# Retention's last transposes eight filler steps later, and a PSUM bank for the value products in layer 1's last stage

## The chip, the cores and the metric

The kernel runs on one core of a Trainium2 chip. The metric is the device time of one execution in microseconds; the time before is the median of three runs, 1503.15 us (1498.87 to 1505.15).

The core has five engines, each with an instruction stream of its own: TensorE (PE in the profile; its weight loads are PEld), VectorE (DVE), ScalarE (ACT), GpSimd (POOL), and SyncE (SP), which here issues nearly all DMA transfers. An engine that comes to an instruction whose inputs or whose buffer is not ready waits, and what stands behind it on that engine waits too. TensorE writes its results to PSUM, eight banks here of 128 x 512 floats; VectorE or ScalarE must take a result out ("evacuate" it) before the bank can serve again.

## What is computed

A two-layer encoder trunk over 1,024 prompt tokens and 512 sample tokens, width 1,024, in float32. Layer 0 has two mixers side by side: dense attention (8 heads, 2 key/value heads, with rotary positions) and retention (4 heads, forward and backward scan over 128-token chunks). Layer 1 is windowed attention (16 heads, tokens within 128 of each other, a relative-position bias and a sink logit). Each branch is multiplied by a SiLU gate and goes through one output projection to the residual.

```python
def attn_retention_layer(x, g, w_in, qk_gain, ret_decay, w_out):
    z = rmsnorm(x, g) @ w_in
    qa, ka, va, ga, qb, kb, vb, gb = jnp.split(z, cuts, axis=-1)
    ...
    oa = dense_gqa(qa, ka, va)
    fwd = retention(qb, kb, vb, log_gamma[0], True)
    bwd = jnp.flip(retention(jnp.flip(qb, 1), jnp.flip(kb, 1), jnp.flip(vb, 1), log_gamma[1], False), 1)
    ob = rmsnorm(fwd + bwd, None)
    mixed = jnp.concatenate([jax.nn.silu(ga) * oa, jax.nn.silu(gb) * ob], axis=-1)
    return x + mixed @ w_out

def windowed_layer(x, g, w_in, sink, rel_bias, w_out):
    z = rmsnorm(x, g) @ w_in
    q, k, v, gate = jnp.split(z, [...], axis=-1)
    o = banded_sink_gqa(q, k, v, sink, rel_bias)
    return x + (jax.nn.silu(gate) * o) @ w_out
```

## The kernel before

**Tiling.** The 1,536 tokens are 12 blocks of 128 (`NB`): blocks 0 to 7 are the prompt, 8 to 11 the sample. Four blocks are a group `t` (`GB` = 4, `NG` = 3), worked on in the order 2, 0, 1 (`ORDER`). Activations stand transposed in SBUF as `X["h", k, t]` and `X["l", k, t]`, a rounded high part and the remainder, for each of 8 slices `k` of the model width; a float32 product is made of three products of such parts. Every matmul is issued by the helper `mm` at line 89, every transpose by line 173, so the profile tells them apart by tiles, not by lines.

**Stages.** Key and value projections; retention, head by head; layer 0's attention; layer 0's output projection, begun inside the attention's last units; layer 1's key/value projection; layer 1's attention; layer 1's output projection, begun in the same way. The last two are what "layer 1's last stage" means below: it lies from about 1299 us on.

**Retention.** `retention(h, w, b0, b1)` projects and rotates a head's queries, keys and values and returns `retain`, which is called one step later as `last()`: it runs the scan over the chunk states (`stt`), and for each group of four blocks makes the products `po` (line 644 on), ScalarE squares them (`sq`), VectorE sums the squares (`ssa`, line 650), GpSimd raises to the power -1/2 (`rstd`, line 103), VectorE scales (`on`, line 653), TensorE transposes (`pto`), ScalarE copies (`oT`, line 658) and SP stores it in HBM. The last `retain`, of head 3 on the sample, is `tail`, and is called inside the attention, by `begin`.

**Fillers.** Both attentions run in `pipeline`: for each unit (a block of queries for four heads) `front` makes scores (`s` in layer 0, `sc` in layer 1) and softmax weights; `Back.T` transposes the weights (`pte`) and splits them (`eh`, `el`); `Back.PV` makes the value products (`po`). Between them `Fill.step` puts in fillers, pieces of projections that are independent of the attention. In layer 0 they are first the query projections of heads 4 to 7 (`q_pieces_a`): eight pieces fill one PSUM tile `psq` for a pair of blocks, and with the eighth the pair's rope step is written: copies on ScalarE (line 479), a sum of squares and three wide passes on VectorE (lines 425, 427, 433, 434), a power and two products on GpSimd (lines 103, 430), and stores. Then come the gates (`psg`), and in each layer's last stage the output projection (`pso`, in `out_proj_fm`): 24 matmuls into one PSUM tile, then `y`, VectorE's addition of the residual (line 283), which evacuates it.

`begin` is called by `pipeline` when the first unit's scores are written: it writes `PRE_A` = 23 fillers, then `tail()`, then `POST_A` = 2.

**PSUM banks.** Five of the eight banks are one ring with the tag `s` (scores, transposes, retention's `po` and `pto`); the other three have the tags `pj0` to `pj2` and are given out by `ps_p` in turn, to fillers (`use="fill"`) and to the value products (`use="out"`):

```python
    ring = dict(all=[0, 1, 2], fill=[0, 1, 2], out=[0, 1, 2], i=0)

    def ps_p(name, use="fill"):
        free = ring[use]
        ring["i"] = next(i % 3 for i in range(ring["i"] + 1, ring["i"] + 4) if i % 3 in free)
        return pp.tile([P, 512], F32, tag=f"pj{ring['i']}", name=name, bufs=1)
```

In layer 0's attention `fill` is `[0, 1]` and `out` is `[2]`; in layer 1 all three serve both.

**What sets the order.** The program is written once, in the order of the code, and a scheduler (the tile framework's, with a model of times) then puts each engine's instructions into the order in which they run: of those that it holds to be ready, the one written first, and `tc.high_priority()` lifts a few. A tile that draws on a ring of buffers must wait for the earlier user of its buffer. A filler that `paced` writes also keeps behind an earlier `pte`.

Of the kernel before, what the change touches and what calls it, by code (L numbers as in the profile page):

```python
# [10 lines left out]
AF = mybir.ActivationFunctionType  # L11
# [11 lines left out]
GB = 4  # L23
# [5 lines left out]
PRE_A = 23  # L29
# [7 lines left out]
def trunk_kernel(ctx, tc, x, xT, wab, woab, wc, woc, gT, qkg, ret, sink, relb, fng,  # L37
                 ropeA, ropeB, dist, kdist, qdist, onehot, wmask, out_p0, out_p1, out_s):
    nc = tc.nc
    dma = nc.sync.dma_start  # L40
# [12 lines left out]
    def buf(tag, name, n=None, dt=F32):  # L53
        t = wk.tile([P, SIZE[tag]], dt, tag=tag, name=name, bufs=BUFS[tag])
        return t if n is None else t[:, :n]
# [4 lines left out]
    def ps_t(name):  # L60
        return pp.tile([P, 512], F32, tag="s", name=name, bufs=5)

    ring = dict(all=[0, 1, 2], fill=[0, 1, 2], out=[0, 1, 2], i=0)
# [9 lines left out]
    def small(name, n, bufs=2):  # L73
        return st.tile([P, n], F32, tag=name, name=name, bufs=bufs)
# [13 lines left out]
    def mm(ps, lhsT, rhs, start, stop):  # L88
        i = nc.tensor.matmul(ps, lhsT=lhsT, rhs=rhs, start=start, stop=stop)  # L89
        if pace["after"] is not None:  # L90
            tc.add_manual_dep(i.ins, pace["after"], order, reason="a filler keeps to its place in the pipeline")
            pace["after"] = None
        return i
# [78 lines left out]
    def transpose(o, i):  # L172
        return nc.tensor.transpose(o, i, ident)  # L173
# [145 lines left out]
    def drain(gens):  # L319
        while gens:  # L320
            for _ in gens.pop():
                pass
# [30 lines left out]
    def scratch(name):  # L353
        return [[dr.tile([P, 512], F32, name=f"{name}{k}{t}")[:] for t in range(NG)] for k in range(KT)]

    o_ab, g_ab, o_c, g_c = scratch("oab"), scratch("gab"), scratch("oc"), scratch("gc")
# [210 lines left out]
    def v4(t):  # L567
        return t.rearrange("p (b i) -> p b i", b=GB)
# [65 lines left out]
    def retain(h, b0, n, parts, tiles, stt, kvs):  # L634
        for i in range(n - 1):
            nc.vector.scalar_tensor_tensor(stt[0:64, i + 1, :], stt[0:64, i, :], cdec[0:64, h:h + 1],
                                           kvs[i // GB][0:64, i % GB, :], ALU.mult, ALU.add)
            j = n - 1 - i
            nc.vector.scalar_tensor_tensor(stt[64:128, j - 1, :], stt[64:128, j, :], cdec[64:128, 4 + h:5 + h],
                                           kvs[j // GB][64:128, j % GB, :], ALU.mult, ALU.add)  # L640
        for i0, (vs, qfb, sT) in zip(parts, tiles):
            po = ps_t("po")
            pov = v4(po)
            for j in range(GB):
                mm(pov[:, j, :], sT[:, j, :], vs[j], True, False)
                mm(pov[:, j, :], qfb[:, j, :], stt[:, i0 + j, :], False, True)
            sq = buf("O", "sq")
            nc.scalar.activation(sq, po, AF.Square)
            ss = small("ssa", 8)[:, :GB]
            nc.vector.tensor_reduce(ss, v4(sq), AX.X, ALU.add)  # L650
            r = rstd_of(ss, P, GB)
            on = v4(buf("O", "on"))
            nc.vector.tensor_tensor(on, pov, r.unsqueeze(2).to_broadcast([P, GB, P]), ALU.mult)
            pt = ps_t("pto")
            for j in range(GB):
                transpose(v4(pt)[:, j, :], on[:, j, :])
            oT = buf("H", "oT")
            nc.scalar.activation(oT, pt, AF.Copy)
            dma(out=o_ab[4 + h][(b0 + i0) // GB], in_=oT)

    def bias_table():
        oh = buf("H", "oh")
# [8 lines left out]
        dma(out=brow_d, in_=wm[:16])  # L671
        dma(out=btab_d, in_=bass.AP(brow_d.tensor, brow_d.offset, [[512, 16], [0, P], [1, 512]]))

    tail = lambda: None
    for h in range(4):
        w = ws[h]
        if h < 3:
            ws.append(load_w(wab, h + 1, "w" if h % 2 else "wg"))
        for (b0, b1) in SEQS:
            tail, last = retention(h, w, b0, b1), tail  # L680
            last()
            if 1 <= 2 * h + (b0 > 0) <= NB // 2:
                q_late(PAIRS[2 * h + (b0 > 0) - 1])

# [210 lines left out]
    fill = Fill(fill_a(), 240 / 110.0)  # L895

    def begin():
        for _ in range(PRE_A):
            fill.one()
        tail()  # L900
        for _ in range(POST_A):
            fill.one()

# [32 lines left out]
    for i in (1, 0):  # L936
        KH, KL, V = seq_tiles(F32R, "KH", "KL", "V")
        for t in ORDER:
            pt = ps_t("ptk")
# [143 lines left out]
    def hook_c(u):  # L1083
        c, b = u
        if c == 3 and b in (BLOCKS[GB], BLOCKS[2 * GB]):
            t = 2 if b == BLOCKS[GB] else 0
            for _ in fillc.gates:
                pass
            if t == 2:
                late.clear()  # L1090
            drain(ahead)
            drain([mix_fm(t, KS_C if t else KS_C[6:], o_c, g_c)])
            ahead.append(mix_fm(0 if t else 1, KS_C[:6], o_c, g_c))
            fillc.more.append(out_proj_fm(t, woc, KS_C, lambda k: x1T_d[k][t], x2T_d, fin_out, None if t else late, nc.vector, t == 0))
# [2 lines left out]
             lambda kb, n: 4 if kb == n - 1 else 0, lambda n: 3.5, fillc, hook_c)  # L1097
    drain(ahead)
    fillc.rest()

    fn = buf("S4", "fn")
    dma(out=fn, in_=bcast(fng, D))
# [103 lines left out]
```

## Time and profile before

| | |
|---|---|
| median of three runs | 1503.15 us |
| lowest, highest | 1498.87, 1505.15 us |
| profiled execution, its own time | 1498.49 us |
| profiled execution, span | 1496.4 us |
| TensorE, share of the span busy | 96% |
| VectorE | 70% |
| GpSimd | 54% |
| ScalarE | 48% |

The profiled execution is a single one, shorter than the median of the runs by 4.7 us; the durations of the rows below are of it alone. A row of the timeline merges neighbouring instructions of one kind (x4); its duration runs from the first's start to the last's end, and since matmuls overlap in the pipeline, the start of the next row, and not the end of this one, tells how long TensorE was taken up. In brackets stands the idle time of the engine ahead of the row and what ended it. A wait in the view of waits is such idle time, summed for one pair of a waiting tile and its releaser.

### The profile page before, as it was taken

The numbers are of one execution on the slowest core, as the hardware profiler recorded it, in microseconds if no ns is written. First come the engines' busy times: TensorE is split into PE (matmuls) and PEld (weight loads), VectorE is DVE, ScalarE is ACT, GpSimd is POOL, SyncE is SP. The second block draws the span as 40 slices with busy tenths as digits, with TensorE's granted clock in tenths as the row PEclk, the third lists the DMA queues.
The fourth block names the chain that finished last, engine by engine and source line by source line (L and its number), as shares of the span: only waits on it lengthen the run. The fifth ranks groups of instructions, "written<-read, shape, count | busy, mean of one in ns | idle before, by whom it ended". The sixth has DMA issues, their size and how long they took to land.

```text
span 1496.4 us, 25439 instructions
## 1 busy us (share of the span) xinstructions
PE 1444.0 (96%) x8446; PEld 1250.3 (84%) x8446; DVE 1050.6 (70%) x2431; ACT 722.8 (48%) x1782; POOL 813.0 (54%) x1044
## 2 busy tenths in 40 slices
PE   8999999999999999989998999999999999999997
PEld 6899999977888887878777998888888888776787
DVE  6466776686666667877978137687777767888774
ACT  5542232364555555555652245565555556645202
POOL 7654664474646575886986433442622532566552
PEclk9999999999999999999999999999999999999999
DMA  9541221326212243543664231221212211567752
GB/s 327 186 147 53 79 57 61 100 74 198 75 50 63 62 119 125 199 142 106 201 207 142 71 119 37 61 78 47 78 40 92 67 51 54 171 209 261 247 166 98
DMA packets 138355, 176.55 MB, mean 118 GB/s; under 512 B 38064, under 2 KB 68784, under 8 KB 138224
## 3 DMA queue, kind: packets, MB, share of 16 engines
q1 hardware_dynamic: 136064, 169.41, 35.9%
q0 software_dynamic: 2016, 5.51, 1.2%
q8 instruction: 67, 1.10, 0.3%
q14 instruction: 64, 0.52, 0.1%
q10 hardware_dynamic: 144, 0.01, 0.0%
HBM read 125.83 MB, written 53.25 MB: 120 GB/s over the span
## 4 chain that ended last, share of the span: by engine, by line
PE 75%; DVE 9%; DMA 6%; POOL 4%; issue 3%; ACT 2%; SPq 0%; POOLq 0%; DVEq 0%; ACTq 0%
PE psg L89 17%; PE psq L89 11%; PE pso L89 9%; PE po L89 9%; PE psb L89 8%; PE pte L173 7%; PE s L89 4%; PE sc L89 4%; PE pskv L89 2%; DVE xl L118 2%; PE pskq L89 2%; DVE w L140 1%; DMA mo<-gab 1%; DMA wraw<-in_woc 1%; PE ptq L173 1%
## 5 line engine op out<-in xcount | busy, mean ns | idle before, releaser
L89 PE MATMUL psg<-xh,wg 128*128 128x512 f32 x768 | 263.4, 400 | 0.4 <-POOL wg L139 0.4
L107 POOL TENSOR_SCALAR ec<-ec,rl 128x384 f32<-128x384 f32 (+1 forms) x192 | 107.9, 576 | 242.3 <-DVE rl L1068 86.3
L112 DVE TENSOR_TENSOR el<-pte,eh 128x512 fp32r<-128x512 f32 x288 | 196.5, 685 | 56.0 <-ACT eh L111 32.4
L111 ACT ACTIVATE eh<-pte 128x512 fp32r<-128x512 f32 x288 | 169.7, 596 | 116.2 <-PE po L89 64.5
L89 PE MATMUL pso<-xh,w 128*128 128x512 f32 x512 | 179.3, 409 | 8.4 <-DVE w L140 3.2
L89 PEld LDWEIGHTS psg<-xh,wg 128*128 128x128 f32 x768 | 143.6, 188 | 28.5 <-POOL wg L139 0.8
L107 POOL TENSOR_SCALAR e<-e,rl 128x512 f32<-128x512 f32 x160 | 117.1, 744 | 87.2 <-DVE rl L860 28.4
L89 PE MATMUL psg<-xl,wg 128*128 128x512 f32 x384 | 150.8, 393 | 0.0
L1063 ACT ACTIVATE ec<-ec,nm 128x384 f32<-128x384 f32 (+1 forms) x192 | 109.6, 572 | 82.3 <-DVE nm L1061 77.4
L857 ACT ACTIVATE e<-s,nm 128x512 f32<-128x512 f32 x160 | 108.8, 686 | 70.8 <-DVE nm L854 51.2
L849 DVE TENSOR_REDUCE nm<-s 128x1 f32<-128x512 f32 x160 | 107.6, 682 | 36.6 <-PE s L89 36.2
L89 PE MATMUL psq<-xh,w 128*128 128x512 f32 x384 | 129.9, 397 | 0.6 <-DVE oT L719 0.6
L139 POOL TENSOR_SCALAR w<-wraw 128x512 fp32r<-128x512 f32 x112 | 75.9, 679 | 90.3 <-PE pskv L89 32.0
L89 PEld LDWEIGHTS pso<-xh,w 128*128 128x128 f32 x512 | 96.7, 192 | 32.9 <-DVE w L140 5.7
L1057 DVE CUSTOM_DVE_ANT_0 ec<-sc,bias,sink_s 128x384 f32<-128x384 f32 (+1 forms) x192 | 105.2, 569 | 22.1 <-PE sc L89 18.2
L89 PE MATMUL pso<-xl,w 128*128 128x512 f32 x256 | 102.5, 402 | 1.6 <-DVE xl L118 1.6
L173 PE MATMUL pte<-ident,e 128*128 128x128 f32 x640 | 95.2, 274 | 1.5 <-ACT e L857 1.3
L173 PEld LDWEIGHTS pte<-ident,e 128*128 128x128 f32 x640 | 78.6, 141 | 19.8 <-ACT e L857 2.9
L140 POOL TENSOR_TENSOR w<-wraw,w 128x512 fp32r<-128x512 f32 x64 | 84.6, 1325 | 1.7
L89 PEld LDWEIGHTS psq<-xh,w 128*128 128x128 f32 x384 | 71.9, 188 | 14.3 <-PE po L89 0.8
L89 PEld LDWEIGHTS psg<-xl,wg 128*128 128x128 f32 x384 | 72.3, 188 | 13.1
L173 PE MATMUL pte<-ident,ec 128*128 128x128 f32 x512 | 78.9, 272 | 0.1
(234 smaller groups left out, 3891.7 us busy)
## 6 DMA issues: line engine op xcount, KB each, us to landing
wraw<-in_woab SPq DMA_DIRECT2D x48, 256.0 KB, 3.3
wraw<-in_woc SPq DMA_DIRECT2D x48, 256.0 KB, 3.9
wraw<-in_wab SPq DMA_DIRECT2D x44, 256.0 KB, 3.4
wraw<-in_wc SPq DMA_DIRECT2D x36, 256.0 KB, 3.1
xt<-in_xT SPq DMA_DIRECT2D x24, 256.0 KB, 5.7
xb<-in_x SPq DMA_DIRECT2D x24, 256.0 KB, 4.0
qd<-qd SPq DMA_DIRECT2D x48, 128.0 KB, 3.0
gab<-gz SPq DMA_DIRECT2D x24, 256.0 KB, 2.0
```

The costliest lines, as they stand in the source:

```text
L89: i = nc.tensor.matmul(ps, lhsT=lhsT, rhs=rhs, start=start, stop=stop)
L107: nc.gpsimd.tensor_scalar(o, i, s, 1.0, ALU.mult, ALU.mult)
L111: nc.scalar.activation(hi, src, AF.Copy)
L112: nc.vector.tensor_tensor(lo, src, hi.bitcast(F32), ALU.subtract)
L118: nc.vector.scalar_tensor_tensor(lo, src, scale, hi.bitcast(F32), ALU.mult, ALU.subtract)
L139: nc.gpsimd.tensor_scalar(w[:, 0, :], raw, 1.0, 1.0, ALU.mult, ALU.mult)
L140: (lo or nc.gpsimd).tensor_tensor(w[:, 1, :], raw, w[:, 0, :].bitcast(F32), ALU.subtract)
L173: return nc.tensor.transpose(o, i, ident)
L849: nc.vector.tensor_reduce(nm2[:, c:c + 1] if nh == 2 else nm[:, h:h + 1], s, AX.X, ALU.max, negate=True)
L857: nc.scalar.activation(eh[c], ss[c], AF.Exp, bias=nm[:, h:h + 1], accum_out=l[:, h, c:c + 1])
L1057: nc.vector.tensor_tensor_reduce(es[h][:, :nk], s, bias[h][:, bo:bo + nk], 1.0, sink_s[:, 4 * c + h:4 * c + h + 1], ALU.add, ALU.max, mx[: ...
L1063: nc.scalar.activation(es[a][:, :nk], es[a][:, :nk], AF.Exp, bias=nm[:, a:a + 1], accum_out=l[:, a:a + 1])
```

## The change

It has two edits. The first: where `retain` works on one group of four blocks (the sample), it no longer writes the transposes, the copy and the store, but returns a function that does (`flip`); with two groups (the prompt) all is written as before. `begin` writes 15 fillers, `tail()`, eight fillers, the postponed transposes, and the two fillers as before. For the other heads' samples the returned function is called at once.

The second: in `hook_c`, which runs in the first unit of each token group, for head group 3 and the token group behind the sample, the ring is set to `fill=[0, 1]`, `out=[2]`, and back to three for both when the attention and its fillers are done.

```diff
--- before.py
+++ after.py
@@ -638,6 +638,7 @@
             j = n - 1 - i
             nc.vector.scalar_tensor_tensor(stt[64:128, j - 1, :], stt[64:128, j, :], cdec[64:128, 4 + h:5 + h],
                                            kvs[j // GB][64:128, j % GB, :], ALU.mult, ALU.add)
+        done = []
         for i0, (vs, qfb, sT) in zip(parts, tiles):
             po = ps_t("po")
             pov = v4(po)
@@ -651,12 +652,18 @@
             r = rstd_of(ss, P, GB)
             on = v4(buf("O", "on"))
             nc.vector.tensor_tensor(on, pov, r.unsqueeze(2).to_broadcast([P, GB, P]), ALU.mult)
-            pt = ps_t("pto")
-            for j in range(GB):
-                transpose(v4(pt)[:, j, :], on[:, j, :])
-            oT = buf("H", "oT")
-            nc.scalar.activation(oT, pt, AF.Copy)
-            dma(out=o_ab[4 + h][(b0 + i0) // GB], in_=oT)
+            done.append((i0, on))
+            if len(parts) > 1:
+                flip(h, b0, *done.pop())
+        return lambda: [flip(h, b0, *d) for d in done]
+
+    def flip(h, b0, i0, on):
+        pt = ps_t("pto")
+        for j in range(GB):
+            transpose(v4(pt)[:, j, :], on[:, j, :])
+        oT = buf("H", "oT")
+        nc.scalar.activation(oT, pt, AF.Copy)
+        dma(out=o_ab[4 + h][(b0 + i0) // GB], in_=oT)
 
     def bias_table():
         oh = buf("H", "oh")
@@ -671,14 +678,14 @@
         dma(out=brow_d, in_=wm[:16])
         dma(out=btab_d, in_=bass.AP(brow_d.tensor, brow_d.offset, [[512, 16], [0, P], [1, 512]]))
 
-    tail = lambda: None
+    tail = lambda: lambda: None
     for h in range(4):
         w = ws[h]
         if h < 3:
             ws.append(load_w(wab, h + 1, "w" if h % 2 else "wg"))
         for (b0, b1) in SEQS:
             tail, last = retention(h, w, b0, b1), tail
-            last()
+            last()()
             if 1 <= 2 * h + (b0 > 0) <= NB // 2:
                 q_late(PAIRS[2 * h + (b0 > 0) - 1])
 
@@ -895,9 +902,12 @@
     fill = Fill(fill_a(), 240 / 110.0)
 
     def begin():
-        for _ in range(PRE_A):
+        for _ in range(PRE_A - 8):
             fill.one()
-        tail()
+        flips = tail()
+        for _ in range(8):
+            fill.one()
+        flips()
         for _ in range(POST_A):
             fill.one()
 
@@ -1088,6 +1098,7 @@
                 pass
             if t == 2:
                 late.clear()
+                ring.update(fill=[0, 1], out=[2])
             drain(ahead)
             drain([mix_fm(t, KS_C if t else KS_C[6:], o_c, g_c)])
             ahead.append(mix_fm(0 if t else 1, KS_C[:6], o_c, g_c))
@@ -1097,6 +1108,7 @@
              lambda kb, n: 4 if kb == n - 1 else 0, lambda n: 3.5, fillc, hook_c)
     drain(ahead)
     fillc.rest()
+    ring.update(fill=[0, 1, 2], out=[0, 1, 2])
 
     fn = buf("S4", "fn")
     dma(out=fn, in_=bcast(fng, D))
```

Where the two edits move instructions, in the order built from the code:

TensorE, where retention's last products meet their transposes (`po` products, `pto` their transposes, `pte` and `ptq` those of attention weights and queries, `s` scores), before:

```order
L89 MATMUL po<-z,sT 128x128
L89 MATMUL po<-stt,qfb 128x128
L173 MATMUL pto<-ident,on 128x128 x4
L173 MATMUL pte<-ident,e 128x128 x4
L173 MATMUL ptq<-ident,qd 128x128 x4
L89 MATMUL s<-ak,qh 128x512
L89 MATMUL s<-ak,ql 128x512
```

and after:

```order
L89 MATMUL po<-z,sT 128x128
L89 MATMUL po<-stt,qfb 128x128
L173 MATMUL pto<-ident,on 128x128 x4
L173 MATMUL pte<-ident,e 128x128 x4
L173 MATMUL ptq<-ident,qd 128x128 x4
L89 MATMUL s<-ak,qh 128x512
L89 MATMUL s<-ak,ql 128x512
```

Nothing moved here: the transposes follow the products at once in both, and the rows ahead, fillers, are the same too.

VectorE at that place (`ssa` sums of squares, of retention's `sq` and of the fillers' `zq`; `ms` the mean; `on` the scaled product that `pto` transposes), before:

```order
L650 TENSOR_REDUCE ssa<-sq 128x4
L425 TENSOR_REDUCE ssa<-zq 128x8
L100 TENSOR_SCALAR ms<-ssa 128x4
L100 TENSOR_SCALAR ms<-ssa 128x8
L425 TENSOR_REDUCE ssa<-zq 128x8
L100 TENSOR_SCALAR ms<-ssa 128x8
L653 TENSOR_TENSOR on<-po,rstd 128x512
L427 TENSOR_TENSOR zq<-zq,rstd 128x512 x2
L112 TENSOR_TENSOR el<-pte,eh 128x512
```

and after:

```order
L651 TENSOR_REDUCE ssa<-sq 128x4
L425 TENSOR_REDUCE ssa<-zq 128x8
L100 TENSOR_SCALAR ms<-ssa 128x4
L100 TENSOR_SCALAR ms<-ssa 128x8
L425 TENSOR_REDUCE ssa<-zq 128x8 x2
L100 TENSOR_SCALAR ms<-ssa 128x8
L654 TENSOR_TENSOR on<-po,rstd 128x512
L100 TENSOR_SCALAR ms<-ssa 128x8
L427 TENSOR_TENSOR zq<-zq,rstd 128x512 x2
L112 TENSOR_TENSOR el<-pte,eh 128x512
L856 TENSOR_REDUCE nm<-s 128x1
```

One reduction for a filler group (line 425), which stood further up, now stands ahead of `on`, and the group's other passes (lines 427, 433, 434) behind it.

TensorE in layer 1's last stage, at the first two projections of the output (`pso_15933` and `pso_16039`; `po_15967` value products, `sc` scores), before:

```order
L89 MATMUL pso_16039<-xl42_15800,w_15923 128x512
L89 MATMUL pso_15933<-xh42_15799,w_15923 128x512
L89 MATMUL pso_15933<-xh52_15807,w_15923 128x512
L89 MATMUL pso_16039<-xh42_15799,w_15923 128x512
L89 MATMUL sc_16004<-ch0_13657,qs3_15072 128x384
L89 MATMUL po_15967<-eh_15894,cv0_13971 128x512
L89 MATMUL sc_16004<-cl0_13659,qs3_15072 128x384
L89 MATMUL pso_15933<-xl52_15808,w_15923 128x512
L89 MATMUL pso_15933<-xh52_15807,w_15923 128x512
L89 MATMUL pso_16039<-xh52_15807,w_15923 128x512
```

and after:

```order
L89 MATMUL pso_15933<-xl72_15824,w_15928 128x512
L89 MATMUL pso_15933<-xh72_15823,w_15928 128x512
L89 MATMUL po_15967<-eh_15975,cv0_13971 128x512
L89 MATMUL sc_16130<-ch0_13657,qs1_15510 128x384
L89 MATMUL sc_16130<-cl0_13659,qs1_15510 128x384
L89 MATMUL po_15967<-el_15976,cv0_13971 128x512
L89 MATMUL sc_16143<-ch0_13657,qs2_15511 128x384
L89 MATMUL sc_16143<-cl0_13659,qs2_15511 128x384
L89 MATMUL pso_16039<-xh02_15767,w_15913 128x512
L89 MATMUL pso_16039<-xl02_15768,w_15913 128x512
```

Before, the matmuls of the two projections are woven into each other; after, the second begins when the first has ended, two value products and four scores later. From TensorE's instructions near 345 us to those near 1298 us the two orders are the same.

## Rows read from the trace of the kernel before

**Rows 1.** The page's first lines: the span, and each engine's busy time.

```profile
span 1496.4 us, 25439 instructions
...
PE 1444.0 (96%) x8446; PEld 1250.3 (84%) x8446; DVE 1050.6 (70%) x2431; ACT 722.8 (48%) x1782; POOL 813.0 (54%) x1044
```

**Rows 2.** TensorE's waits, whole span: in total, times, longest, all in us.

```profile
PE pto L173 <- DVE on L653: 4.0, 1, 4.0
...
PE po L89 <- DVE y L283: 1.9, 1, 1.9
...
PE pso L89 <- DVE oT L719: 0.9, 1, 0.9
...
PE pso L89 <- DVE y L283: 0.6, 2, 0.3
```

**Rows 3.** Busy time by stretch: length, then PE, PEld, DVE, ACT, POOL; clock; DMA.

```profile
305.00:345.00 40.00, 38.53 (x236) 32.54 (x235) 37.79 (x83) 26.41 (x64) 30.03 (x36) 1.00 0.32 87
1290.00:1330.00 40.00, 34.83 (x155) 27.31 (x154) 39.08 (x87) 22.49 (x56) 28.25 (x30) 0.91 0.73 238
1320.00:1330.00 10.00, 7.82 (x23) 5.62 (x24) 9.66 (x20) 4.02 (x7) 5.38 (x7) 0.66 0.68 213
```

**Rows 4.** Timeline of TensorE: start, us, instruction, [idle before it <- releaser].

```profile
286.20 0.60 PE L173 MATMUL pto<-ident,on 128*128 128x128 f32 x4
...
301.97 1.12 PE L173 MATMUL pto<-ident,on 128*128 128x128 f32 x4 [3.98 <-DVE on L653]
```

**Rows 5.** Timeline of VectorE, the retention's end and behind it.

```profile
283.85 0.69 DVE L425 TENSOR_REDUCE ssa<-zq 128x8 f32<-128x512 f32 x1 [0.37 <-ACT zq L423]
...
301.22 0.69 DVE L653 TENSOR_TENSOR on<-po,rstd 128x512 f32<-128x512 f32 x1 [0.28 <-POOL rstd L103]
...
319.69 0.69 DVE L112 TENSOR_TENSOR el<-pte,eh 128x512 fp32r<-128x512 f32 x1 [1.24 <-ACT eh L111]
```

**Rows 6.** Timeline of GpSimd, beside it.

```profile
300.16 4.24 POOL L103 TENSOR_TENSOR rstd<-ms,nhalf 128x4 f32<-128x4 f32 x3 [1.48 <-DVE ms L100]
```

**Rows 7.** Timeline of TensorE, layer 1's last stage, first part.

```profile
1316.30 0.39 PE L89 MATMUL pso<-xh,w 128*128 128x512 f32 x1
...
1318.12 0.39 PE L89 MATMUL pso<-xh,w 128*128 128x512 f32 x1
...
1323.01 0.76 PE L89 MATMUL po<-eh,cv 128*128 128x512 f32 x1 [1.85 <-DVE y L283]
...
1327.97 1.05 PE L89 MATMUL pso<-xh,w 128*128 128x512 f32 x2
...
1330.66 0.62 PE L89 MATMUL pso<-xh,w 128*128 128x512 f32 x2
1331.11 0.39 PE L89 MATMUL pso<-xl,w 128*128 128x512 f32 x1
```

**Rows 8.** Timeline of VectorE there: the evacuations `y` of five projections.

```profile
1322.17 0.69 DVE L283 TENSOR_TENSOR y<-pso,y 128x512 f32<-128x512 f32 x1
...
1324.88 0.68 DVE L283 TENSOR_TENSOR y<-pso,y 128x512 f32<-128x512 f32 x1
...
1355.66 0.68 DVE L283 TENSOR_TENSOR y<-pso,y 128x512 f32<-128x512 f32 x1
...
1369.01 0.68 DVE L283 TENSOR_TENSOR y<-pso,y 128x512 f32<-128x512 f32 x1
...
1378.19 0.68 DVE L283 TENSOR_TENSOR y<-pso,y 128x512 f32<-128x512 f32 x1
```

**Rows 9.** Timeline of TensorE, second part of that stage.

```profile
1351.00 0.39 PE L89 MATMUL pso<-xh,w 128*128 128x512 f32 x1
...
1362.62 0.39 PE L89 MATMUL pso<-xh,w 128*128 128x512 f32 x1
...
1368.46 1.04 PE L173 MATMUL pte<-ident,ec 128*128 128x128 f32 x8
...
1374.15 0.40 PE L89 MATMUL pso<-xh,w 128*128 128x512 f32 x1
```

## The prediction

> **What bounds the kernel now.** I read the page first: TensorE is busy 1444.0 of 1496.4 us [rows 1], so a gain can only come from its idle time and from stretches where it runs at the lower clock. The view of TensorE's waits comes next; the reader is to look for the waits that the two edits name. The longest single one of a transpose is retention's `pto`, 4.0 us behind VectorE's `on`; then come `po` behind `y` with 1.9, `pso` behind `oT` with 0.9 and `pso` behind `y` with 0.6 in two waits [rows 2]. The first belongs to edit 1; 1.9, 0.9 and one 0.3 of the 0.6 belong to the last stage of layer 1, edit 2. Last, the busy times by stretch. From 305 to 345 us VectorE works 37.79 of 40 us, and from 1290 to 1330 39.08 of 40 [rows 3]: behind both places VectorE is nearly as full as TensorE, so what is taken from a TensorE wait there may be met again as a wait for VectorE.
>
> **Edit 1: the transposes eight fillers later.** The code asks for 15 fillers, products, 8 fillers, transposes. The built order does not give that: on TensorE `po` and `pto` still stand next to each other, and what stands ahead of them is the same. The scheduler places what is ready, and the fillers are ready before the products. So the 3.98 us of idle ahead of `pto` stay, and so does the lower clock behind it: four transposes take 1.12 us there against 0.60 at 286.20 [rows 4]. Nothing is removed.
>
> What does move is the vector work of one filler group (the rope step of the second pair of query blocks). It stood on VectorE from 283.85 on, in a stretch with room; now it stands behind retention's sum of squares, since the group's last filler is written after the products, and both draw `ssa` tiles from one ring of two, which I take to be the reason. It is four wide instructions of about 0.69 us (the first at 283.85) and one tiny one: 4 x 0.69 = 2.8 us, on VectorE; on GpSimd a power `rstd` of 4.24 / 3 = 1.4 us [rows 5, 6] and two products. Its two stores to HBM leave SP's queue earlier in order and enter it later; the loads `qd` behind them come sooner, and none of the transposes that wait for `qd` near there is late by more than 0.3 us.
> - Ahead of `on` stands one more reduction of 0.69 us; VectorE had 0.28 us of idle there [rows 5]. `on` and `pto` come 0.69 - 0.28 = 0.4 us later. That is a loss.
> - The rest, 2.8 - 0.7 = 2.1 us, falls into the full stretch from 305. The cover is VectorE's own holes, 40 - 37.79 = 2.2 us [rows 3], of which one of 1.24 lies at 319.69 [rows 5], and TensorE's fillers, which the new order draws ahead of the scores. If the holes take it all it costs 0; without cover 2.1. I take 0.6, nearer to the first, since a hole of 1.24 follows within 15 us.
> - Below nothing: VectorE is freer from 284 to 292, but TensorE loses only 0.3 us there. Bound -0.3.
>
> Sum of edit 1: 0.4 + 0.6 = **+1.0 us**, bounds -0.3 and +2.5.
>
> **Edit 2: the bank of its own.** Taken away: the value products `po` wait no more for a projection's evacuation (1.9), nor the projections `pso` for a value product's (0.9), and the 0.3 at 1325.70 sits in the same chain: 1.9 + 0.9 + 0.3 = 3.1 us [rows 2]. With the idle goes the lower clock that follows it: from 1320 to 1330 the granted clock is 0.66 [rows 3], a mix of the two levels, 2.4 and 1.2 GHz. Two products `pso` take 1.05 us at 1327.97 and 0.62 at 1330.66 [rows 7], 0.2 us more each; 13 products lie between 1323.01 and 1329.2, eleven at 0.2 and two narrow ones at 0.15: 2.5 us. Together 5.6 us.
>
> Added: the code's ring gives out the next free number. With projections on 0 and 1 and value products on 2, the number after 2 is 0. So a projection that follows a value product always gets bank 0, and bank 1 is used only where two projections follow each other. Of the first eight projections one gets bank 1. Each other must wait until VectorE has added its forerunner into `y`; the built order agrees, for `pso_16039`, woven into `pso_15933` before, now begins after it. In the trace of before the evacuation comes late, since it stands in line on VectorE: the last product of the first projection starts at 1316.30 (0.39 us long), its `y` at 1322.17, and the product that it holds at 1323.01, 0.84 later [rows 7, 8]. So a bank is free 1323.01 - 1316.69 = 6.3 us after its last product. For the next ones, last product's end to `y` plus 0.84: 1318.51 to 1325.72, 7.2 us; 1351.39 to 1356.50, 5.1; 1363.01 to 1369.85, 6.8; 1374.55 to 1379.03, 4.5 [rows 7 to 9].
>
> The cover is what the new order puts on TensorE in between. A wide product takes 0.23 us of it (two from 1330.66 to 1331.11 [rows 7]), a transpose 1.04 / 8 = 0.13 [rows 9], and a narrow score product I count as 0.18. Behind the first: two `po`, four scores, 1.2 us. Behind the second: two scores, 12 transposes, four `po`, eight projections, 4.7. Behind the third the fourth, on bank 1, fills the time, and I count no wait. Behind the fifth, sixth and seventh (`pso_16380`, `pso_16535`, `pso_16672`): 2.8, 3.1 and 1.0. Uncovered: 5.1 + 2.5 + 2.3 + 3.7 + 3.5 = 17.1 us if VectorE is as late as before; 0 if each `y` comes within its cover. I take 7: VectorE's order is new too. Walking it with before's durations from the point where the two orders part (1305.3), with 0.6 us from the start of one wide row to the next, the first `y` ends near 1319, about 2 us behind the end of its projection's cover instead of 5.1, some 40%; 0.4 x 17.1 = 7.
>
> Sum of edit 2: 7 - 5.6 = **+1.4 us**, bounds 0 - 5.6 = -5.6 and 17.1 - 3.1 = +14.0 (a new wait keeps the clock low).
>
> **A rule that speaks against it.** The row first: `y` of the first projection starts 5.5 us after the product it needs, in a stretch in which VectorE idles 0.9 us of 40 [rows 3, 8]. The Trainium skill, "TensorE: Matmul & The Clock Gate", table of specifications at its head, has VectorE's queue as strictly first in, first out; the trace agrees. By that rule alone the evacuation always waits out the rows ahead of it, which would be 17.1 in the place of my 7, and edit 2 at +14.0 or, with the clock back, +11.5. That is the second rival below.
>
> **The sum.** +1.0 + 1.4 = +2.4 us. The profiled execution took 1498.49 us (span 1496.4 and 2.1 around it), 4.7 below the median of the runs, 1503.15; on it the sum gives 1500.9, on the median 1505.5. I predict **1505.5 us**.
>
> **The rivals.**
> - *A gain.* Nothing new is waited for, since each `y` comes within its cover: 1.0 - 5.6 = -4.6, 1498.5 us. For it: in all the rest of the kernel, where layer 0's last stage already has its banks split so, `pso` waits for `y` 0.3 us once [rows 2]. Against it: there two projections follow one value product, so both banks are used. Chance 0.20.
> - *The one bank becomes the bound.* The new waits stay as late as before's evacuations: 1.0 - 3.1 + 17.1 = +15, near 1518 us. It is slower by over 7.5 us once the five waits come to 7.5 - 1.0 + 5.6 = 12.1 us, 2.4 each. For it: VectorE at 39.08 of 40. Against it: it is less full from 1330 on. Chance 0.13.
> - *The moved rope work holds TensorE.* Edit 1 at its bound of 2.5 and the wait followed by as much again at the lower clock, some +5, with edit 2 as forecast: +6.4, 1509.5. Decides if VectorE has no hole between 302 and 345. Chance 0.10.
> - *Edit 1 does what it says.* `pto` would wait for nothing: -4.0 and some 2 us of clock, +1.4: -4.6, 1498.5. The order speaks against it; 0.03.
>
> **How the numbers follow.** Forecast 0.54, its own range 1500 to 1510. 0.5% is 7.5 us, about what a measurement of this kernel can tell from no change. Slower by more: 0.12 of the second rival, 0.03 of the third, 0.03 of the forecast's upper edge: 0.18. Faster by more: a quarter of the first, and 0.01 of the last: 0.06. Within: 0.76. The range runs from 1497, just under the first rival, to 1512, short of the second: about 0.2 is left out.
>
> **What would show it.** Edit 1: TensorE's waits still list `pto` behind `on`, at 4.0 to 4.6 us; VectorE from 305 to 345 is at 39 or more of 40. If `pto` is gone from the waits, the order was misread. Edit 2: `po` behind `y` is gone; `pso` behind `y` has grown from 0.6 to some 7 us in about five waits, the first near 1318; the clock from 1320 to 1330 is nearer to 1. With `pso` behind `y` under 2 us the first rival holds; over 12 us the second. A change of over 3 us between 350 and 1290 us, where the order is the same, would overturn the whole.

## The result, and the profile after

| | before | after |
|---|---|---|
| median | 1503.43 us (4 runs) | 1516.06 us (4 runs, 1511.67 to 1519.11) |
| ratio to before, 95% interval | | 1.0095 (1.0077 to 1.0112) |
| profiled execution, its own time | 1498.49 us | 1511.67 us |
| profiled execution, span | 1496.4 us | 1509.6 us |

The change made the kernel 0.95% slower, about 14 us, where I had forecast +2.4 us and a range up to 1512 us. The two profiled executions differ by 13.2 us.

TensorE's waits of the changed kernel, whole span (total, times, longest, in us), the rows that answer to [rows 2]:

```profile
PE pso L89 <- DVE y L283: 6.7, 3, 3.2
...
PE pso L89 <- POOL w L139: 5.0, 2, 3.9
...
PE pto L173 <- DVE on L654: 4.1, 1, 4.1
...
PE po L89 <- DVE qs L118: 1.5, 1, 1.5
```

`pto` still waits 4.1 us for `on`, as predicted: edit 1 moves nothing on TensorE. `po` behind `y` is gone. `pso` behind `y` came to 6.7 us, close to the 7 that I had named, but by luck: 5.4 of it lie behind the attention, where I had forecast none. And there are two waits that I had not priced: `po` behind `qs`, 1.5 us, and `pso` behind GpSimd's `w`, which grew. In before it read:

```profile
PE pso L89 <- POOL w L139: 3.7, 4, 2.0
```

Busy time by stretch after (columns as in [rows 3]; the last row is a stretch that was not shown of before):

```profile
305.00:345.00 40.00, 36.94 (x217) 30.26 (x216) 38.08 (x76) 24.57 (x59) 30.81 (x36) 0.98 0.31 85
1290.00:1330.00 40.00, 34.49 (x162) 26.14 (x161) 37.95 (x89) 23.70 (x60) 26.54 (x31) 1.00 0.74 243
1320.00:1330.00 10.00, 9.23 (x40) 6.83 (x40) 9.96 (x25) 6.58 (x17) 6.30 (x9) 1.00 0.69 231
1330.00:1400.00 70.00, 61.87 (x283) 49.12 (x282) 50.32 (x119) 31.80 (x80) 42.83 (x48) 0.95 0.74 235
```

and the last stretch in before:

```profile
1330.00:1400.00 70.00, 65.36 (x318) 51.38 (x317) 56.09 (x128) 34.54 (x86) 45.84 (x53) 1.00 0.78 257
```

The clock from 1320 to 1330 us rose from 0.66 to 1.00, as edit 2 was meant to bring. But between 1330 and 1400 us, later than the place that I looked at, TensorE lost 3.5 us of busy time and its clock fell from 1.00 to 0.95. From 305 to 345 us TensorE lost 1.6 us of busy time.

Where the time came from, by the starts of the same instruction in both timelines: at `pto`, 301.97 before and 301.04 after, the new execution is 0.9 us ahead; at a score's exponential on ScalarE near 357 us it is 2.3 behind; at the first scores' exponential of layer 1's attention, 901.93 and 906.90, 5.0 behind; at the one near 1298 us 4.2 behind; at the end 13.2. The 0.9 us at `pto` are not the change's: they are there from 231 us on, ahead of all that it moves. The first step, 3.2 us, lies at edit 1, and the last, 9 us, at edit 2; the first comes out alike in the traces of two runs below that have edit 1, 3.4 us in e1_flip and 3.3 in g4_after_act. The 2.7 us between 357 and 902 lie where the instruction order is unchanged; of the runs below with the same order there, e8_sixteen is 3.7 us longer than before between these two rows and g1_serial 2.3 shorter, so I count them as scatter of single executions. That is why the shares of the two edits are taken from separate timed runs.

### The profile page after: what moved, and what is told of

It is laid out like the page before. It is cut to its first block, busy times and chain, and to the rows that moved or that the text cites. A ratio compares the mean times of both kernels' runs of the same rounds, so it can differ in the third digit from the quotient of the medians.

```text
span 1509.6 us, 25443 instructions
## 1 busy us (share of the span) xinstructions
PE 1445.5 (96%) x8446; PEld 1251.5 (83%) x8446; DVE 1048.2 (69%) x2431; ACT 723.0 (48%) x1782; POOL 809.6 (54%) x1044
## 4 chain that ended last, share of the span: by engine, by line
PE 73%; DVE 10%; DMA 7%; POOL 4%; issue 4%; ACT 2%; SPq 0%; POOLq 0%; DVEq 0%; ACTq 0%
PE psg L89 17%; PE psq L89 10%; PE psb L89 8%; PE po L89 8%; PE pso L89 7%; PE pte L173 6%; PE pskq L89 4%; PE s L89 4%; PE sc L89 3%; PE pskv L89 2%; DVE xl L118 2%; DMA wraw<-in_woc 1%; DVE w L140 1%; DVE el L112 1%; PE ptq L173 1%
## 5 line engine op out<-in xcount | busy, mean ns | idle before, releaser
L89 PE MATMUL psg<-xh,wg 128*128 128x512 f32 x768 | 263.4, 400 | 0.0
L89 PE MATMUL pso<-xh,w 128*128 128x512 f32 x512 | 178.6, 406 | 12.0 <-DVE y L283 5.4
L89 PEld LDWEIGHTS psg<-xh,wg 128*128 128x128 f32 x768 | 143.6, 188 | 28.0 <-POOL wg L140 0.3
L89 PE MATMUL psg<-xl,wg 128*128 128x512 f32 x384 | 150.8, 393 | 0.0
L89 PE MATMUL psq<-xh,w 128*128 128x512 f32 x384 | 130.0, 397 | 0.0
L89 PEld LDWEIGHTS pso<-xh,w 128*128 128x128 f32 x512 | 96.9, 191 | 33.2 <-POOL w L139 9.1
L89 PE MATMUL pso<-xl,w 128*128 128x512 f32 x256 | 102.5, 400 | 3.5 <-DVE xl L118 3.5
L89 PEld LDWEIGHTS psq<-xh,w 128*128 128x128 f32 x384 | 71.9, 188 | 13.6
L89 PEld LDWEIGHTS psg<-xl,wg 128*128 128x128 f32 x384 | 72.3, 188 | 13.0
```

## The experiments

Each was timed in several rounds beside the kernel before on the same chip; the ratio is to that kernel, with its 95% interval, and us are the ratio's excess times 1503.

**Each edit alone.** e1_flip has edit 1 only, e2_bank edit 2 only.

> Edit 1 alone. Theory A (edit 1 moves rope work behind retention's tail and makes the waits near 320 to 345 us longer): 3 us slower than before, ratio 1.002, and TensorE's wait of pto for on is still there at 4 us. Rival B (the 3 us between 302 and 345 us are chance of one execution): ratio 1.000. Rival C (edit 1 carries most of the loss): ratio 1.006 or more.

Measured: 1.0026 (1.0012 to 1.0039), +3.9 us.

> Edit 2 alone. Theory A (edit 2 carries the larger part of the loss): 9 us slower, ratio 1.006; projections pso wait for evacuations y for 5 us in all after the last attention unit, near 1400 to 1430 us. Rival C (edit 1 carries most): ratio 1.003 or less.

Measured: 1.0044 (1.0027 to 1.0060), +6.6 us. The waits of `pso` for `y` behind the attention were 4.8 us. Both edits cost, the second more; the two sum to 10.5 us, and the whole change has 14.3; the intervals (of about 2, 2.5 and 2.6 us to either side) allow that difference.

**Edit 1: is it the moved rope step?** e8_sixteen:

```diff
-        for _ in range(PRE_A - 8):
+        for _ in range(PRE_A - 7):
             fill.one()
         flips = tail()
-        for _ in range(8):
+        for _ in range(7):
             fill.one()
```

> Edit 1 alone, but 16 fillers ahead of retention's tail and 7 behind it, instead of 15 and 8: the second filler group is then complete, and its rope step written, ahead of the tail; on TensorE the built order is that of before. Theory A (edit 1 costs because one group's rope step moves from ahead of the tail to behind it): the 3.9 us of edit 1 alone go, ratio 1.000. Rival B (something else of edit 1 costs, such as the transposes written later): ratio 1.0026 as with edit 1 alone.

Measured: 1.0004 (0.9992 to 1.0017). With one filler more ahead of the tail the loss is gone. The transposes are still written later than in before, but by its trace the rows of TensorE, VectorE, ScalarE and GpSimd follow one another as in before from start to end. So what cost was the sixteenth filler alone, whose rope step fell behind the tail, and what the scheduler made of that.

**Edit 1: would a true distance have paid?** e9_held16 is e8_sixteen, and the seven fillers carry an ordering dependence on retention's last product:

```diff
         for _ in range(7):
+            pace["after"] = last_po[0]
             fill.one()
+        pace["after"] = None
```

> Edit 1 as its words say: 16 fillers, retention's products, 7 fillers that TensorE may not begin before these products, then the transposes. TensorE has some 8 us of filler between products and transposes. Theory A (the wait of 4 us and the lower clock behind it can be had back by a true distance): the wait of pto for on goes, 4 to 6 us faster, ratio 0.997. Rival E (the fillers are then missing as cover a little later, and VectorE's full stretch takes it back): ratio 1.000.

Measured: 1.0026 (1.0015 to 1.0038), slower, which neither expectation had. TensorE's timeline there (start, us, instruction, [idle before it <- releaser]):

```profile
293.06 0.77 PE L173 MATMUL ptq<-ident,qd 128*128 128x128 f32 x4 [3.45 <-DMA qd<-qd]
...
304.47 0.60 PE L173 MATMUL pto<-ident,on 128*128 128x128 f32 x4
```

`pto` waits for nothing and runs at the full clock (0.60 us), so the edit as its words say does remove the wait. But the fillers that now stand behind the products are missing ahead of them, where they had covered the load of `qd`: 0.29 us of wait for it in before (at 291.59) became 3.45. TensorE's waits from 255 to 300 us:

```profile
PE ptq L173 <- DMA qd<-qd: 3.5, 1, 3.5
PE psq L89 <- DVE sT L629: 2.1, 1, 2.1
PE psq L89 <- ACT zq L479: 0.9, 1, 0.9
```

That is 6.5 us, where before waits 0.5 there, and from 284 to 300 us the granted clock is 0.89 in the place of 1.00. So more is lost ahead of the products than the 4.0 us that are saved behind them. Laid beside before, the run is 0.9 us behind at 260 us, 2.5 at `pto` and 5.2 at the score's exponential near 357; I did not take that last part apart.

**Edit 2: the two banks behind the attention, or bank 0 again and again?** e3_restore sets the ring back to three banks ahead of the remaining projections; e4_turns lets projections take 0 and 1 strictly in turn:

```diff
+    ring.update(fill=[0, 1, 2], out=[0, 1, 2])
     drain(ahead)
     fillc.rest()
-    ring.update(fill=[0, 1, 2], out=[0, 1, 2])
```

```diff
         free = ring[use]
+        if len(free) == 2 and ring.get("alt"):
+            ring["f"] = 1 - ring.get("f", 1)
+            return pp.tile([P, 512], F32, tag=f"pj{ring['f']}", name=name, bufs=1)
```

> Edit 2 alone, but the ring goes back to three banks as soon as the attention's last unit is written, ahead of the remaining projections and not behind them. Theory A (what costs is that the remaining projections, which come without value products, have two banks instead of three): the 5 us of waits of pso for y and the lower clock behind them go, 2 to 3 us slower than before, ratio 1.002. Rival D (what costs is that each projection behind a value product gets bank 0, inside the attention): as edit 2 alone, ratio 1.006.

> Edit 2 alone, but projections take banks 0 and 1 strictly in turn, whatever the value products took; the ring goes back to three banks behind the remaining projections, as in edit 2. Theory A (the remaining projections with two banks): hardly better than edit 2 alone, ratio 1.005. Rival D (bank 0 given out again and again): the loss goes, ratio 1.000 or under, down to 0.997 where the waits that edit 2 removed, some 5 us, come out as a gain.

Measured: e3_restore 1.0039 (1.0026 to 1.0052), e4_turns 1.0058 (1.0042 to 1.0075). Neither idea held. In e3_restore the waits for `y` behind the attention fell from 4.8 to 0.3 us, and GpSimd's and VectorE's `w` took their place, 3.9 us. TensorE's waits there, behind 1400 us:

```profile
PE pso L89 <- POOL w L139: 2.5, 4, 1.4
PE pso L89 <- DVE w L140: 1.4, 2, 1.1
...
PE pso L89 <- DVE y L283: 0.3, 1, 0.3
```

In e4_turns the waits for `w` shrank, and value products and projections met their banks. TensorE's waits from 1290 us to the end (the edit moves the lines by three, so L92 is L89 of before):

```profile
PE pso L92 <- DVE y L286: 8.6, 4, 4.7
PE po L92 <- ACT xh L120: 4.7, 1, 4.7
PE po L92 <- DVE oT L722: 3.5, 3, 1.7
PE pso L92 <- POOL w L142: 1.3, 2, 0.8
```

`po` behind `oT` is a value product that waits for the one bank of its own, 3.5 us in three waits. The 4.7 us behind ScalarE's `xh` I did not follow up. With the weights prepared by GpSimd, two banks and one serve this stage worse than three in common, whichever way the two are given out.

**Edit 2: the first wait.** e11_swap is edit 2 with `fill=[1, 2], out=[0]`.

> Edit 2 alone with other bank numbers: value products on 0, projections on 1 and 2. The first value product of the stage then does not follow the last query projection in its bank, which in edit 2 it has to wait for (po behind qs, 1.5 us near 1313). Theory H (that first wait sets off the rest of the loss): ratio 1.002 or less. Rival G (the loss comes from the later waits): ratio 1.004 as with edit 2 alone, or 1.003 where only the 1.5 us go.

Measured: 1.0043 (1.0027 to 1.0058). The wait behind `qs` does not set off the rest: it is gone in this trace, and the loss is the same. What stands there in its place are waits for the weights' low part on VectorE, 4.1 us from 1290 to 1400, and two of the waits for `y` that I had forecast. TensorE:

```profile
1361.33 0.50 PE L89 MATMUL pso<-xh,w 128*128 128x512 f32 x1 [2.41 <-DVE y L283]
...
1373.22 0.47 PE L89 MATMUL pso<-xh,w 128*128 128x512 f32 x1 [1.74 <-DVE y L283]
```

So which wait ends last in this stage hangs on the numbers of the banks, while the time hardly does.

**Edit 2: the weights.** The trace of the changed kernel shows the longest new wait of TensorE in this stage behind GpSimd. TensorE:

```profile
1381.99 0.80 PE L89 MATMUL pso<-xh,w 128*128 128x512 f32 x1 [3.90 <-POOL w L139]
```

GpSimd ahead of it (`w` is the high part of the next weights, `mo` a gate product, `ec` the softmax weights' scaling):

```profile
1352.96 0.62 POOL L139 TENSOR_SCALAR w<-wraw 128x512 fp32r<-128x512 f32 x1 [0.29 <-DMA wraw<-in_woc]
...
1363.64 1.29 POOL L262 TENSOR_TENSOR mo<-mo 128x512 f32<-128x512 f32 x1 [5.19 <-DMA mo<-oc]
...
1370.10 1.04 POOL L139 TENSOR_SCALAR w<-wraw 128x512 fp32r<-128x512 f32 x1
```

and in before:

```profile
1356.21 0.63 POOL L139 TENSOR_SCALAR w<-wraw 128x512 fp32r<-128x512 f32 x1 [1.90 <-PE pso L89]
...
1361.28 0.62 POOL L139 TENSOR_SCALAR w<-wraw 128x512 fp32r<-128x512 f32 x1
...
1367.51 1.05 POOL L139 TENSOR_SCALAR w<-wraw 128x512 fp32r<-128x512 f32 x1
```

Before, GpSimd prepares three weights between 1356 and 1368 us, the first as soon as its buffer is free (it waits for a `pso`). After, it prepares none for 17 us, from 1352.96 to 1370.10. Two things hold this `w` up. Its buffer is still read, by the built order, until the product that starts at 1362.76:

```profile
1362.76 0.62 PE L89 MATMUL pso<-xh,w 128*128 128x512 f32 x2
```

And then it stands in GpSimd's queue behind the `mo` that waited 5.19 us for its load and the rows that follow that. It is not yet the weight that TensorE waits for at 1381.99. That one is the second behind it; its load needs a buffer that becomes free only when the weight of 1370.10 is prepared, and takes 8.2 us to land. SyncE, then GpSimd:

```profile
1372.95 0.33 SPq L135 DMA_DIRECT2D wraw<-in_woc  x1
```

```profile
1381.32 0.62 POOL L139 TENSOR_SCALAR w<-wraw 128x512 fp32r<-128x512 f32 x1 [1.91 <-DMA wraw<-in_woc]
```

e10_act_w takes the copy out of GpSimd's queue, in edit 2 alone; f1_before_act_w does the same in before, as a control:

```diff
-            nc.gpsimd.tensor_scalar(w[:, 0, :], raw, 1.0, 1.0, ALU.mult, ALU.mult)
+            if lo is None:
+                nc.gpsimd.tensor_scalar(w[:, 0, :], raw, 1.0, 1.0, ALU.mult, ALU.mult)
+            else:
+                nc.scalar.activation(w[:, 0, :], raw, AF.Copy)
```

(`lo` is given in layer 1's last stage and in the closing projection of either layer, so both kernels have the copy moved there too.)

> Edit 2 alone, with one more change in the weight loads of the output projections: the high part w is copied by ScalarE instead of GpSimd. Theory F (in edit 2 the projections lose their time to weights that arrive late, since their conversion stands on GpSimd behind a product mo that waits 5 us for its load): the waits of pso for GpSimd's w, 3.6 us near 1380, go, and 4 us or more of edit 2's 6.6 come back, ratio 1.002 or less. Rival G (the weights are late by their loads, or the loss lies elsewhere): ratio 1.004 or more.

> The kernel before, with the high part w of the output projections' weights copied by ScalarE instead of GpSimd: the control for the run that had edit 2 and this. Theory F (edit 2 loses because its weights come late from GpSimd): without that, edit 2 shows what it removes and adds at the banks, and this control is no faster than edit 2 with the same copy, ratio 0.995 to 0.998. Rival G (the copy on ScalarE helps both alike, and edit 2 still loses its 6 us): ratio 0.991.

Measured: edit 2 with the copy on ScalarE 0.9954 (0.9939 to 0.9969), before with it 0.9956 (0.9942 to 0.9969). The move is worth 13.5 us to edit 2 and 6.6 us to before, and with it edit 2 costs nothing that these runs could tell: 0.0002 between the two. The copy itself is no faster there: 0.632 us at the median on ScalarE, 0.624 on GpSimd. What counts is the queue in which it stands; whether the wait of `mo` or GpSimd's other rows hold it up more was not tested. TensorE's waits from 1345 to 1400 us in e10_act_w:

```profile
PE pso L89 <- DVE y L286: 3.0, 2, 2.6
PE sc L89 <- DVE mx L1060: 1.9, 3, 0.8
PE pte L176 <- POOL ec L107: 1.5, 2, 1.3
```

No wait for `w` is left, and the wait that I had predicted for edit 2, of `pso` for `y` inside the attention, now appears, 3.0 us.

**Why are the weights late?** Two projections share their weights. In the built order of the changed kernel the first pair runs one behind the other, where in before it is woven product by product. So a weight stays in use longer: laid beside the traces, the built order has the stage's first weight buffer in use from 1299.52 to 1308.26 us in before, and from 1302.92 to 1325.64 after (starts of the first and the last product that read it). g1_serial takes such an order alone, for the first four pairs (the third and fourth stand so in before already), with before's three banks:

```diff
                 for kk in ks:
+                    if lo is not None and t == 2 and a and kk == ks[0]:
+                        pace["behind"] = end
                     proj_fm_k(ps, w, a * P, t, kk, ks)
                     if kk != ks[-1]:
                         yield
+                end = pace["last"]
```

where `mm` makes its product follow `pace["behind"]` and keeps its own name in `pace["last"]`.

> The kernel before with its three common banks, and one thing of edit 2 alone: on TensorE the second projection of each pair that shares its weights begins only behind the last product of the first, for the first four pairs (in before the first pair is woven, product by product, and the second in changed order). Theory J (in edit 2 the projections run one behind the other, hold the four weight buffers longer, and so the next weights come late from GpSimd): ratio 1.003 to 1.006, and pso waits for GpSimd's w for 3 us or more between 1345 and 1400 us. Rival K (the order of the projections is not it; the banks' waits and the value products' shift are): ratio 0.998 to 1.001.

Measured: 1.0071 (1.0056 to 1.0087), +10.7 us, with no bank touched. That is more than I had expected, and more than edit 2; the second pair, which is partly interleaved in edit 2 too, is put in line here as well, which may be why. TensorE's waits from 1345 to 1400 us:

```profile
PE pso L89 <- POOL w L142: 5.7, 3, 3.8
PE pso L89 <- DVE w L143: 2.9, 3, 2.1
```

against, in before:

```profile
PE pso L89 <- DVE w L140: 1.8, 3, 0.8
...
PE pso L89 <- POOL w L139: 0.5, 1, 0.5
```

g2_serial_act is g1_serial with the copy on ScalarE.

> The kernel before with the first four pairs of projections one behind the other, as in the run before, and w copied by ScalarE. Theory J (the order of the projections costs only because GpSimd then delivers the next weights late): the 10 us of the run before go, ratio 0.9945 to 0.9965, as the control with w on ScalarE, which had 0.9956. Rival L (the order costs by itself): ratio 1.000 or more.

Measured: 0.9958 (0.9942 to 0.9974), the control's value. So the order costs through the weights that GpSimd prepares, and nothing else of it that these runs could tell.

**What a better version looks like.** f2_act_restore is e10_act_w with three banks behind the attention; f3_act_turns_restore adds the turns of e4_turns; g4_after_act is the whole change with the copy on ScalarE.

> Edit 2 with w copied by ScalarE, and the ring back at three banks as soon as the attention's last unit is written. Edit 2 with w on ScalarE alone has 1.4 us of waits of pso for y behind the attention: ratio 0.994 to 0.9955, at most 2 us from 0.9954.

> As the run before it, and projections take banks 0 and 1 strictly in turn. If bank 0 given out again and again is what is left of the loss (3.0 us of waits of pso for y inside the attention), ratio 0.992; if the value products then wait for their one bank instead, as with w on GpSimd, ratio 0.997 or more.

> Both edits with w copied by ScalarE. If the two edits' costs are separate, edit 1's 1.0026 is left on 0.9954: ratio 0.998. If edit 1's loss also hangs on GpSimd's weights: 0.9955.

Measured: f2_act_restore 0.9949 (0.9933 to 0.9966), f3_act_turns_restore 0.9992 (0.9980 to 1.0004), g4_after_act 0.9989 (0.9977 to 1.0001). The first beats both kernels, by 7.7 us against before, but is not told apart from the control f1_before_act_w. The turns lose 6.5 us again. In the last, edit 1's cost is left as it was alone: 0.9989 less 0.9954 is 0.0035, beside its 0.0026. The two edits' losses are separate, and neither edit adds a gain to the copy's move.

## Why the prediction was wrong

**Edit 1, what it does: right.** The built order kept `po` and `pto` together, `pto` waited 4.1 us, and what moved was one group's rope step. e8_sixteen shows that the cost goes when it does not move.

**Edit 1, its size: the term of the full stretch was mis-sized.** I took 0.6 of 2.1 us for it, because a hole of 1.24 us on VectorE followed within 15 us, and +1.0 (-0.3 to +2.5) for the edit. It measured +3.9 (1.8 to 5.9). The other term, 0.4 us for a later `on`, came to 0.1: the wait of `pto` grew from 3.98 to 4.06. What was missing is the chain behind VectorE: the vector work stood ahead of a score's row maximum `nm`, ScalarE's exponential came late, and the transposes of the weights waited for it 30 us further on. ScalarE in before, and after:

```profile
332.86 0.69 ACT L857 ACTIVATE e<-s,nm 128x512 f32<-128x512 f32 x1 [4.17 <-DVE nm L854]
```

```profile
334.47 0.69 ACT L864 ACTIVATE e<-s,nm 128x512 f32<-128x512 f32 x1 [5.54 <-DVE nm L861]
```

TensorE after:

```profile
335.31 0.66 PE L173 MATMUL pte<-ident,e 128*128 128x128 f32 x4 [1.54 <-ACT e L864]
...
337.19 0.66 PE L173 MATMUL pte<-ident,e 128*128 128x128 f32 x4 [0.32 <-DVE el L112]
...
341.71 0.50 PE L89 MATMUL po<-el,av 128*128 128x512 f32 x1 [0.81 <-DVE el L112]
```

In before two waits stood there:

```profile
333.69 1.32 PE L173 MATMUL pte<-ident,e 128*128 128x128 f32 x8 [0.67 <-ACT e L857]
...
342.33 0.50 PE L89 MATMUL psg<-xh,wg 128*128 128x512 f32 x1 [0.41 <-POOL wg L139]
```

With the last small one after, 0.2, that makes 2.9 against 1.1, +1.8 us. In e1_flip the waits there come to 3.2 us, in e8_sixteen to 1.2. VectorE from 305 to 345 is at 38.08 of 40, not the 39 or more that I named: not its total decided, but which row it held up. In this pair of traces there is also the clock behind `pto`. In before TensorE is back at the full clock 3.4 us after the wait's end; after, a pair of query products is still slow (0.63, where 0.39 is usual) 4.3 us after it:

```profile
305.37 0.63 PE L89 MATMUL psq<-w,xh 128*128 128x256 f32 x2
...
306.57 0.40 PE L89 MATMUL psq<-w,xh 128*128 128x256 f32 x2
```

and in before:

```profile
305.38 0.39 PE L89 MATMUL s<-ak,qh 128*128 128x512 f32 x1
```

By 306.9 us both traces stand at the same row, though after had been 0.9 us ahead at `pto`: 1 us lost. 1.8 and 1.0 make 2.8 of the 3.2 us that this place cost in the trace. But that 1.0 can't be put down to edit 1. In runs with edit 2 alone or part of it the rows here are those of before, and the full clock came back between 3.1 us (f2_act_restore) and 6.0 us (e4_turns) behind the same wait:

```profile
304.95 1.12 PE L176 MATMUL pto<-ident,on 128*128 128x128 f32 x4 [3.98 <-DVE on L656]
...
308.00 0.40 PE L89 MATMUL s<-ak,ql 128*128 128x512 f32 x1
```

```profile
303.38 1.11 PE L176 MATMUL pto<-ident,on 128*128 128x128 f32 x4 [3.97 <-DVE on L656]
...
308.77 0.41 PE L92 MATMUL psq<-w,xl 128*128 128x256 f32 x1
...
309.38 0.28 PE L92 MATMUL psq<-w,xl 128*128 128x256 f32 x1
```

So of edit 1's +3.9 us the trace accounts for 1.8 to 2.1 by waits; the rest is open.

**Edit 2, what it removes: right.** The waits of `po` for `y` and of `pso` for `oT` went, and the clock came back (0.66 to 1.00 from 1320 to 1330).

**Edit 2, what it adds: the wrong wait.** The step that failed is the added term, "17.1 us if VectorE is as late as before", of which "I take 7": five waits of `pso` for `y` inside the attention. None appeared there. The order covered them: three of the projections begin 0.74 or 0.75 us behind the start of the `y` that frees their bank (1324.38 behind 1323.64, 1361.47 behind 1360.73, 1388.60 behind 1387.85), just when TensorE came to them. TensorE's waits from 1345 to 1400 us after:

```profile
PE pso L89 <- POOL w L139: 3.9, 1, 3.9
PE sc L89 <- DVE el L112: 1.1, 1, 1.1
PE pte L173 <- POOL ec L107: 0.9, 2, 0.7
```

Inside the seventh projection (`pso_16672`) TensorE met another resource: the four weight buffers. I had read from the order that `pso_16039` now begins behind `pso_15933` and had priced the bank in that, but not that the two share their weights. A pair one behind the other keeps each weight buffer until the second has used it; then the next weights are prepared late, and GpSimd, which prepares them, has other rows in its queue by then. g1_serial put a price on that order alone, +10.7 us, and with the copy on ScalarE (g2_serial_act) it cost nothing. My sum has no term for the weights.

The two-bank wait behind the attention, `pso` for `y` 5.4 us after 1400, was missing from the sum too: the ring goes back to three banks only behind the remaining projections. Cured (e3_restore) it gave next to nothing; waits for the weights took its place.

**The rivals.** The second, near 1518 us, came closest in time (1516.06), but by luck: its waits of `pso` for `y` inside the attention are not in the trace. What did cost was a queue all the same, GpSimd's, in which the copy of `w` stands behind other rows, and not VectorE's. The Trainium skill ("TensorE: Matmul & The Clock Gate", table of specifications) has both queues as strictly first in, first out; the traces agree. With the copy out of that queue, my sum has edit 2 at 1.4 us of loss and the runs at -0.3 us, with some 3 us of uncertainty; the trace of e10_act_w has 4.4 us of waits for `y` (3.0 inside the attention, 1.4 behind it) where I had taken 7. So the sum agrees with a kernel in which the weights don't bind, as far as these runs can tell. The last rival, edit 1 as its words say, had some 6 us of gain from edit 1 (4.6 with edit 2 as forecast); by e9_held16 such an edit loses 3.9. I had left out what the moved fillers had covered.

**What stays open.** Why GpSimd's order changed so that `mo` stands ahead of `w`: whether by the weight buffers' later release or by the scheduler's model of the value products was not told apart. Nor how much of the late weights is the held buffer, GpSimd's rows, or the slower load; moving the copy changes all three. Nor where the 3.8 us between the whole change and the sum of its edits lie; scatter would do.

## What to carry to other kernels

When a change gives two streams of work their own buffers, ask of each stream what else it holds while it waits: here two projections that share weights, put one behind the other, kept the weight buffers and delayed the next weights, which cost more here than the banks. Look at the queue of an engine that prepares inputs for the critical one, and at what stands ahead of them there, rows that wait for loads above all: moving 64 copies of 0.62 us from GpSimd to ScalarE was worth 6.6 us, at the same duration of the copy. And when fillers are moved to cover one wait, look at what they cover now; and when they are counted out, count to the end of a group, since a group's last piece brings its vector work with it.

## What the runs showed of the hardware

The lower clock behind one and the same wait did not last equally long from one execution to the next: behind 3.97 to 3.98 us of idle time and the same rows TensorE was at full clock 3.1 us later in f2_act_restore (308.00), 3.4 in before (305.38) and 6.0 in e4_turns (309.38). A single trace therefore can't price what the lower clock costs behind such a wait to better than some 1.5 us (an estimate: half of the 2.9 us between the two, since the lower clock is half of the full one).

A copy of 128 x 512 floats took 0.62 us on GpSimd and 0.63 on ScalarE. The Trainium skill ("GPSIMD Engine Reference", section 4.1, Engine selection) has GpSimd, set beside VectorE, at roughly line rate for work with one input; no run here has this copy on VectorE.
